# Prompt state of an mLSTM mixer in chunks of two token tiles, and v split in two parts where it is made

## Chip, cores and metric

The kernel runs on one core of one Trainium2 chip as a single launch. The metric is device time in microseconds (us), the median of several executions. TensorE (PE) multiplies matrices, VectorE (DVE), ScalarE (ACT) and GpSimd (POOL) work on elements, and SyncE (SP) issues most DMA transfers; ACT issues some.

## What is computed

Two layers in f32 over 1024 prompt frames and 8 sample streams of 16 frames, with 1024 model features and an inner width of 2048. Layer 0 is a gMLP-style mixer (A), layer 1 an xLSTM mLSTM block (B) of 4 heads of 512. The change is in mixer B, whose core the reference computes chunk by chunk, with a state C (512 x 512 per head) that is carried on:

```python
q, k, v = blockdiag(xc, wq), blockdiag(xc, wk), blockdiag(xm, wv)
...
s = jnp.einsum('bhtd,bhsd->bhts', q, k) * w_intra
num = jnp.einsum('bhts,bhse->bhte', s, v) + w_inter[..., None] * jnp.einsum('bhtd,bhde->bhte', q, C)
den = jnp.sum(s, axis=-1) + w_inter * jnp.einsum('bhtd,bhd->bht', q, n)
h = num / jnp.maximum(jnp.abs(den), jnp.exp(-m_t))[..., None]
...
C_new = decay[..., None, None] * C + jnp.einsum('bhs,bhsd,bhse->bhde', w, k, v)
n_new = decay[..., None] * n + jnp.einsum('bhs,bhsd->bhd', w, k)
```

Then h is layer-normed, gated by silu(z), and projected back with w_out. Outputs are the frames of both batches and the new states (C, n, m, conv) of both. The length of a chunk is free for the result: a longer chunk moves work from "q times C" to "scores times v".

## The kernel before

**Precision.** Most products are made in three matmuls (mm3) from two parts of each operand: `split(hi, lo, x, eng)` casts x to hi on ACT (L89) and subtracts on DVE or, where named, on POOL (L90). A scores block is a plain f32 matmul, which stands as two records in the profile.

**Stages.** 0 to 820 us: mixer A. 852 to 1147: the feature stage, 16 features of 3 steps; a step makes, for 384 tokens, the inner feature (xmp), the convolution and silu (xc), v in token order (`values`, PSUM tile pvv), q and k, and stores v, skip*xc, q and k into DRAM tensors (vb_d, sk_d, q_d, k_d), all issued by ACT. 1147 to 1173: gate section (rA, transposes with ident). 1173 to 1405: the matmuls of z with the first sample streams. 1405 to 1960: the rest of the unit stage.

**Unit stage.** 36 units: 4 heads x (8 prompt tiles of 128 tokens, and one tile with the 128 sample tokens, a "rider" that shares the iteration of a prompt unit). For a prompt tile n of head h an iteration runs, in PE's order: the two halves (a = 0, 1; 258 and 256 columns) of the numerator, scores times v (`va,s`) and, for n > 1, the scaled q times the state (`Ch,q`, `Cl,q`); the state update k times v (`va,k`) in 4 row blocks c and 2 halves; the scores and transposed k of the next tile (`qT,kT`, `ident,kT`); the output projection of the tile two before (`w,o`, whose sum into the residual x is L1380, on DVE); transposes of the normalised output (`ident,hn`). Between them stand the sample streams: for each of 8 samples and 4 heads a state of 512 x 512 comes from DRAM (c), is read by q (`c,qT`), gets a rank-48 update (`sk`, from the DRAM tensor st_d, which `Dec.keys` writes) and goes back. cw holds the gate weights of a tile; it is loaded by partition broadcast (L1037), and `mask` (L1211) is its first reader.

**State.** Tile 0's update waits for tile 1: these two are already one chunk (k0, `parts`, sO, the tile 1 terms of the code). From tile 2 on each tile is a chunk of its own: Cst = Cst * decay + update (L1278 on DVE, 8 times a tile), and `settle` splits Cst into Ch and Cl, a row block at a time, by ACT with DVE or POOL in turn. v is loaded as f32 (vv) and split into va by `prep_v` (ACT, then POOL). `scale_q` (L1252) multiplies q by the carried-state weight.

**Order.** PE executes in the order of the program; the order on the other engines is set by the scheduler. Buffers: 3 va tiles, 2 k2, one sO (in the q2 pool), one Cst, Ch and Cl.

Of the kernel before, what the change touches and what calls it, by code (L numbers as in the profile page):

```python
# [15 lines left out]
P = 128  # L16
# [7 lines left out]
H = 4  # L24
# [46 lines left out]
def trunk_kernel(ctx: ExitStack, tc: tile.TileContext, ins: dict, outs: list):  # L71
# [56 lines left out]
    vb_d = [dram.tile([NT * P, DH], F32, name=f"vb_d{h}") for h in range(H)]  # L128
# [577 lines left out]
    class Feature:  # L706
# [60 lines left out]
        def values(self, b):  # L767
# [8 lines left out]
            st = bw.tile([P, 3, P], F32, name="st", bufs=5)  # L776
            A.copy(out=st, in_=pvv[:, :, :P])
            V.tensor_tensor(out=gtok[:, 3 * b:3 * b + 3], in0=gtok[:, 3 * b:3 * b + 3], in1=pvv[:, :, P:], op=ALU.add)
            A.dma_start(out=vb_d[h].rearrange("(n p) e -> p n e", p=P)[:, 3 * b:3 * b + 3, fs], in_=st)
            sk = bw.tile([P, BT], F32, name="st", bufs=5)  # L780
# [67 lines left out]
    def z_steps():  # L848
        for f in range(NF):
# [3 lines left out]
            for b in range(NB):  # L853
# [3 lines left out]
                st = zs.tile([P, BT], F32, name="st", bufs=5 if zs is bw else 2)  # L857
# [129 lines left out]
    dec8 = const.tile([SB, H], F32, name="dec8")  # L987
    selh = gt.tile([H, H, P], F32, name="selh")
    V.tensor_copy(out=selh, in_=ident[:H, :H].unsqueeze(2).to_broadcast([H, H, P]))
    tpd, tp8 = (ps.tile([P, DH], F32, name="sm") for _ in range(2))  # L990
    for h in range(H):
        T.matmul(tpd[:, 16 * h:16 * h + 16], selh[:, h], de16, start=True, stop=True)
    T.transpose(tp8[:SB, :H], de16[:, 8:16], ident[:H, :H])
    V.tensor_copy(out=decB.rearrange("p h c -> p (h c)"), in_=tpd[:, :16 * H])
    V.tensor_copy(out=dec8, in_=tp8[:SB, :H])

    k0 = const.tile([P, H], F32, name="k0")
    V.tensor_tensor(out=k0, in0=tok[:, 0, 1], in1=decB[:, :, 1], op=ALU.mult)
# [19 lines left out]
    def load_qkv(pool, h, n, want, prev=None, bufs=None):  # L1018
# [10 lines left out]
        if "v" in want:  # L1029
            t = pool.tile([P, DH], F32, name="vv")  # L1030
            l = S.dma_start(out=t, in_=vb_d[h][ts, :])
            if prev is not None:
                after(l, prev)
            got["v"] = t
# [17 lines left out]
    class Dec:  # L1052


        def __init__(self, h, prev):
            self.h = h
            self.g = load_qkv(dw, h, 8, ("qT",), prev, bufs=2)
            self.g.update(load_qkv(dw, h, 8, ("cw",), prev))
            self.ev = []
            kv = self.kv = rawp.tile([P, 2, DH], F32, name="raw")  # L1060
            loads = (S.dma_start(out=kv[:, 0].rearrange("p (c t) -> p c t", c=DC), in_=k_d[h].rearrange("(c p) t -> p c t", p=P)[:, :, 8 * P:]),
                     S.dma_start(out=kv[:, 1], in_=vb_d[h][8 * P:, :]))
            for l in loads:
                if prev is not None:
                    after(l, prev)
            self.nn = dw.tile([SB, DH], F32, name="nn")
            S.dma_start(out=self.nn, in_=ins["state_mlstm_n"][0, :, h])
# [5 lines left out]
        def keys(self):  # L1073
# [6 lines left out]
            kp = k_tokens(self.kv[:, 0].rearrange("p (c t) -> p c t", c=DC), ps, "sm")  # L1080
            kw = self.kw = rawp.tile([P, DH], F32, name="raw")
            A.activation(out=kw, in_=kp, func=AF.Copy, scale=tok[:, 8, 1, h:h + 1])
            kv = wp.tile([P, 4, DH], F32R, name="w")
            split(kv[:, 0], kv[:, 1], kw, G)
            split(kv[:, 2], kv[:, 3], self.kv[:, 1], G)
            for r, (kpart, vpart) in enumerate(((0, 2), (0, 3), (1, 2))):
                for q, part in enumerate((kpart, vpart)):
                    S.dma_start(out=f32(st_d[h])[:, r * SL:(r + 1) * SL, q, :], in_=f32(kv)[:, part])
# [4 lines left out]
        def normaliser(self):  # L1093
            h = self.h
            pn = ps.tile([P, DH], F32, name="sm")
            T.matmul(pn[:SB], blk8, self.kw, start=True, stop=True)
            V.scalar_tensor_tensor(out=self.nn, in0=self.nn, scalar=dec8[:, h:h + 1], in1=pn[:SB], op0=ALU.mult, op1=ALU.add)
            A.dma_start(out=n_s[0, :, h, :], in_=self.nn)
# [60 lines left out]
    vas = [me.tile([P, 2, 2, VA], F32R, name=f"va{j}", bufs=1) for j in range(3)]  # L1159
# [8 lines left out]
    class Unit:  # L1168
        def __init__(self, h, n):
            self.h, self.n, self.smp = h, n, n == 8  # L1170
            self.inter = 1 < n < 8
            self.g = {}
# [12 lines left out]
    def scores_pe(u):  # L1185
# [15 lines left out]
        if u.n == 1:  # L1201
# [4 lines left out]
    def mask(u, step):  # L1206
# [5 lines left out]
        else:  # L1212
            e = A.activation(out=u.dd, in_=u.dd, func=AF.Exp, bias=tok[:, u.n, 0, u.h:u.h + 1])
            if u.n == 2:
                after(e, u.before.sO_split)

    def prep_k(u):
# [3 lines left out]
        col = tok[:, u.n, 1, u.h:u.h + 1] if u.n else k0[:, u.h:u.h + 1]  # L1221
# [3 lines left out]
    def prep_s(u):  # L1225
# [7 lines left out]
        if u.n == 1:  # L1233
# [354 lines left out]
```

## Time and profile before

| | before |
|---|---|
| median of 3 runs, us | 1967.85 (1966.57 to 1975.25) |
| profiled execution, us | 1961.52 |
| its span on the core, us | 1959.8 |
| mean granted TensorE clock, share of full speed | 0.986 |
| PE busy, us of the span | 1900.5 (97%) |
| DVE / ACT / POOL busy, us | 1270.3 / 850.0 / 621.4 |
| DMA | 328.21 MB, mean 167 GB/s |

The profile is one execution, so sums are made against its 1961.52 us. PE busy counts matmul records, which overlap in a pipeline; the distance between the starts of two groups is what a group costs.

### The profile page before, as it was taken

What the parts mean: (1) busy time and instruction counts of PE and PEld (TensorE: products, weight loads), DVE (VectorE), ACT (ScalarE), POOL (GpSimd) and SP (SyncE); (2) the same over time, 40 slices, a digit from 0 to 9 for tenths busy, and PEclk for the clock granted to TensorE, in tenths of its full rate; (3) what the DMA queues carried; (4) which work ended last, traced back from release to release, by engine and by line L of the source; (5) the groups of instructions that cost most, each with busy time, mean ns of one, the idle gap of its engine ahead of it and who ended that gap; (6) DMA issues with size and microseconds to landing.
All of it is one profiled execution on the core that took longest, in us unless ns stands there. A gap on an engine that the chain in (4) does not pass through costs nothing.

```text
span 1959.8 us, 32037 instructions
## 1 busy us (share of the span) xinstructions
PE 1900.5 (97%) x11553; PEld 1681.2 (86%) x11553; DVE 1270.3 (65%) x2522; ACT 850.0 (43%) x1727; POOL 621.4 (32%) x637
## 2 busy tenths in 40 slices
PE   7999999999998999989999989999999999999998
PEld 6888999999998788889999959888987787788887
DVE  5822477777776354477667635222498798898897
ACT  5422444444444243455555635112343344344454
POOL 3000244444441000035444401000145435345466
PEclk9999999999999999999999979999999999999999
DMA  6222333333334654335555554687998897775533
GB/s 213 92 92 77 106 98 103 103 103 99 103 98 163 200 170 142 113 99 154 161 162 156 167 152 143 207 259 235 282 306 264 267 284 243 261 239 177 154 122 129
DMA packets 345690, 328.21 MB, mean 167 GB/s; under 512 B 28164, under 2 KB 276948, under 8 KB 345532
## 3 DMA queue, kind: packets, MB, share of 16 engines
q1 hardware_dynamic: 288812, 261.03, 43.3%
q10 hardware_dynamic: 56720, 65.13, 10.6%
q8 instruction: 91, 1.49, 0.3%
q14 instruction: 67, 0.55, 0.1%
HBM read 203.07 MB, written 123.02 MB: 166 GB/s over the span
## 4 chain that ended last, share of the span: by engine, by line
PE 74%; DVE 13%; DMA 7%; ACT 2%; issue 2%; POOL 1%; SPq 1%; ACTq 0%; POOLq 0%; DVEq 0%
PE sm L58 74%; DVE Cst L1278 2%; DMA cw<-cw_d 2%; DVE c L1129 2%; DVE Cl L90 1%; DVE qT L1252 1%; DMA out<-c 1%; DVE raw L1361 1%; DVE bst L1318 1%; DMA c<-in_state_mlstm_C 1%; DMA vv<-vb_d 1%; DMA r<-in_a_w_in 0%; DVE dn L1324 0%; DVE x L1380 0%; DMA st_d<-w 0%
## 5 line engine op out<-in xcount | busy, mean ns | idle before, releaser
L58 PE MATMUL sm<-xh,w 128*128 128x384 f32 x1536 | 410.9, 341 | 4.3 <-DVE w L90 1.5
L58 PEld LDWEIGHTS sm<-xh,w 128*128 128x128 f32 x1536 | 281.5, 189 | 12.8 <-issue 8.2
L58 PE MATMUL sm<-xl,w 128*128 128x384 f32 x768 | 260.4, 339 | 1.1 <-DVE xl L90 1.1
L58 PE MATMUL sm<-Xh,w 128*128 128x288 f32 x1024 | 216.3, 298 | 4.6 <-ACT c L499 4.6
L58 PE MATMUL sm<-w,o 128*128 128x512 f32 x864 | 209.9, 398 | 2.9 <-ACT o L89 1.2
L58 PE MATMUL sm<-w,os 128*128 128x512 f32 x864 | 200.7, 393 | 6.6 <-ACT os L89 6.6
L58 PEld LDWEIGHTS sm<-w,os 128*128 128x128 f32 x864 | 162.9, 190 | 42.8 <-ACT os L89 9.1
L58 PEld LDWEIGHTS sm<-w,o 128*128 128x128 f32 x864 | 159.8, 188 | 41.1 <-ACT hn L1330 1.7
L58 PE MATMUL sm<-w,Xh 128*128 128x512 f32 x576 | 180.2, 394 | 1.8 <-DVE w L90 1.4
L58 PEld LDWEIGHTS sm<-Xh,w 128*128 128x128 f32 x1024 | 168.2, 189 | 5.2 <-ACT c L499 5.0
L90 DVE TENSOR_TENSOR w<-r,w 128x512 fp32r<-128x512 f32 x176 | 136.1, 779 | 50.3 <-ACT w L89 49.8
L58 PE MATMUL sm<-S,w 128*128 128x288 f32 x1152 | 163.8, 297 | 0.0
L90 DVE TENSOR_TENSOR w<-raw,w 128x1024 fp32r<-128x1024 f32 x44 | 56.4, 1281 | 156.8 <-ACT w L89 156.7
L58 PEld LDWEIGHTS sm<-S,w 128*128 128x128 f32 x1152 | 155.1, 188 | 0.8
L58 PE MATMUL sm<-Xl,w 128*128 128x288 f32 x512 | 151.4, 296 | 0.0
L58 PEld LDWEIGHTS sm<-xl,w 128*128 128x128 f32 x768 | 145.1, 189 | 1.3 <-DVE xl L90 1.3
L89 ACT CAST w<-r 128x512 fp32r<-128x512 f32 x176 | 107.3, 618 | 68.8 <-PE sm L58 29.3
L58 PEld LDWEIGHTS sm<-w,Xh 128*128 128x128 f32 x576 | 108.0, 189 | 25.3 <-DVE w L90 2.6
L58 PE MATMUL sm<-w,Xl 128*128 128x512 f32 x288 | 112.6, 391 | 0.0
L90 DVE TENSOR_TENSOR os<-or,os 128x384 fp32r<-128x384 f32 x96 | 53.0, 556 | 90.1 <-ACT os L89 90.1
L58 PE MATMUL sm<-va,k 128*128 128x258 f32 (+1 forms) x768 | 104.5, 286 | 3.4 <-DVE x L1380 1.7
L89 ACT CAST w<-raw 128x1024 fp32r<-128x1024 f32 (+1 forms) x56 | 55.2, 987 | 116.6 <-DMA raw<-in_b_w_in 91.2
(306 smaller groups left out, 3734.5 us busy)
## 6 DMA issues: line engine op xcount, KB each, us to landing
c<-in_state_mlstm_C SPq DMA_DIRECT2D x64, 512.0 KB
out<-c SPq DMA_DIRECT2D x64, 512.0 KB
r<-in_a_w_in SPq DMA_DIRECT2D x96, 256.0 KB
or<-o_d SPq DMA_DIRECT2D x96, 192.0 KB
raw<-in_b_w_in SPq DMA_DIRECT2D x32, 512.0 KB
qT<-q_d SPq DMA_DIRECT2D x40, 256.0 KB
vh<-v_d SPq DMA_DIRECT2D x48, 192.0 KB
vb_d<-st ACTq DMA_DIRECT2D x48, 192.0 KB
```

Source lines behind the costliest of these rows:

```text
L58: ins = fn(*args, **kw)
L89: first = A.copy(out=hi, in_=src)
L90: (lo_eng or V).tensor_tensor(out=lo, in0=src, in1=f32(hi), op=ALU.subtract)
L1129: V.scalar_tensor_tensor(out=c0[:, cc], in0=c0[:, cc], scalar=decB[:, d.h, 8 + b:9 + b], in1=pc, op0=ALU.mult, op1=ALU.add)
L1252: V.tensor_tensor(out=u.g["qT"], in0=u.g["qT"], in1=u.g["cw"][:, 1:2].to_broadcast([P, DC, P]), op=ALU.mult)
L1278: V.scalar_tensor_tensor(out=Cst[:, c, a, :w], in0=Cst[:, c, a, :w], scalar=decB[:, h, n:n + 1], in1=pc, op0=ALU.mult, op1=ALU.add)
L1318: V.bn_stats(out=bst[:, a], in_=hn[:, a, :256])
L1361: V.scalar_tensor_tensor(out=og[:, c], in0=u.pT[:, c], scalar=colB[:, HNG, 4 * h + c:4 * h + c + 1], in1=g["sk"][:, c], op0=ALU.mult, op1= ...
```

## The change

On odd tiles (n = 1, 3, 5, 7) the unit also computes an off-diagonal score block O, this tile's q with the k of the tile before, and adds O times that tile's v to its numerator. The state is updated, and split into Ch and Cl, on odd tiles alone, from both tiles' k and v. So each chunk has two tiles, as tiles 0 and 1 had. q of an odd tile is scaled by the decay of the tile before as well. v is split into its two parts in the feature stage, right out of PSUM (tile sv), stored as two parts (vb_d gets a leading 2) and loaded by two DMAs straight into va, of which there are four; `prep_v` and the vv tile go. `Dec.keys` copies v's parts into st_d without a split. The sample normaliser is made transposed, in n0T, with one final transpose.

```diff
-    vb_d = [dram.tile([NT * P, DH], F32, name=f"vb_d{h}") for h in range(H)]
+    vb_d = [dram.tile([2, NT * P, DH], F32R, name=f"vb_d{h}") for h in range(H)]
...
-            st = bw.tile([P, 3, P], F32, name="st", bufs=5)
-            A.copy(out=st, in_=pvv[:, :, :P])
+            sv = bw.tile([P, 2, 3, P], F32R, name="sv", bufs=2)
+            split(sv[:, 0], sv[:, 1], pvv[:, :, :P])
...
-            A.dma_start(out=vb_d[h].rearrange("(n p) e -> p n e", p=P)[:, 3 * b:3 * b + 3, fs], in_=st)
-            sk = bw.tile([P, BT], F32, name="st", bufs=5)
+            for q in range(2):
+                A.dma_start(out=f32(vb_d[h])[q].rearrange("(n p) e -> p n e", p=P)[:, 3 * b:3 * b + 3, fs], in_=f32(sv)[:, q])
+            sk = bw.tile([P, BT], F32, name="st", bufs=3)
...
-    dec8 = const.tile([SB, H], F32, name="dec8")
...
-    tpd, tp8 = (ps.tile([P, DH], F32, name="sm") for _ in range(2))
+    tpd = ps.tile([P, DH], F32, name="sm")
...
-    T.transpose(tp8[:SB, :H], de16[:, 8:16], ident[:H, :H])
...
-    V.tensor_copy(out=dec8, in_=tp8[:SB, :H])
-    k0 = const.tile([P, H], F32, name="k0")
-    V.tensor_tensor(out=k0, in0=tok[:, 0, 1], in1=decB[:, :, 1], op=ALU.mult)
+    k0 = const.tile([P, 4, H], F32, name="k0")
+    for j in range(4):
+        V.tensor_tensor(out=k0[:, j], in0=tok[:, 2 * j, 1], in1=decB[:, :, 2 * j + 1], op=ALU.mult)
+    dec2 = const.tile([P, H, 4], F32, name="dec2")
+    d2 = decB[:, :, 0:8].rearrange("p h (j i) -> p h j i", i=2)
+    V.tensor_tensor(out=dec2, in0=d2[:, :, :, 0], in1=d2[:, :, :, 1], op=ALU.mult)
...
-            t = pool.tile([P, DH], F32, name="vv")
-            l = S.dma_start(out=t, in_=vb_d[h][ts, :])
-            if prev is not None:
-                after(l, prev)
-            got["v"] = t
+            va = got["v"] = vas[0]
+            vas.append(vas.pop(0))
+            for q in range(2):
+                S.dma_start(out=f32(va)[:, q, :, :256], in_=f32(vb_d[h])[q, ts, :].rearrange("p (a e) -> p a e", a=2))
...
-            kv = self.kv = rawp.tile([P, 2, DH], F32, name="raw")
-            loads = (S.dma_start(out=kv[:, 0].rearrange("p (c t) -> p c t", c=DC), in_=k_d[h].rearrange("(c p) t -> p c t", p=P)[:, :, 8 * P:]),
-                     S.dma_start(out=kv[:, 1], in_=vb_d[h][8 * P:, :]))
+            self.kT = rawp.tile([P, DC, P], F32, name="raw")
+            self.vv = rawp.tile([P, 2, DH], F32, name="raw")
+            loads = (S.dma_start(out=self.kT, in_=k_d[h].rearrange("(c p) t -> p c t", p=P)[:, :, 8 * P:]),
+                     S.dma_start(out=self.vv, in_=f32(vb_d[h])[:, 8 * P:, :].rearrange("q p e -> p q e")))
...
-            self.nn = dw.tile([SB, DH], F32, name="nn")
-            S.dma_start(out=self.nn, in_=ins["state_mlstm_n"][0, :, h])
...
-            kp = k_tokens(self.kv[:, 0].rearrange("p (c t) -> p c t", c=DC), ps, "sm")
-            kw = self.kw = rawp.tile([P, DH], F32, name="raw")
+            kp = k_tokens(self.kT, ps, "sm")
+            kw = self.kw = self.kT.rearrange("p c t -> p (c t)")
...
-            kv = wp.tile([P, 4, DH], F32R, name="w")
+            kv = wp.tile([P, 2, DH], F32R, name="w")
...
-            split(kv[:, 2], kv[:, 3], self.kv[:, 1], G)
-            for r, (kpart, vpart) in enumerate(((0, 2), (0, 3), (1, 2))):
-                for q, part in enumerate((kpart, vpart)):
-                    S.dma_start(out=f32(st_d[h])[:, r * SL:(r + 1) * SL, q, :], in_=f32(kv)[:, part])
+            for r, (kpart, vpart) in enumerate(((0, 0), (0, 1), (1, 0))):
+                for q, src in enumerate((f32(kv)[:, kpart], self.vv[:, vpart])):
+                    S.dma_start(out=f32(st_d[h])[:, r * SL:(r + 1) * SL, q, :], in_=src)
...
         def normaliser(self):
...
-            pn = ps.tile([P, DH], F32, name="sm")
-            T.matmul(pn[:SB], blk8, self.kw, start=True, stop=True)
-            V.scalar_tensor_tensor(out=self.nn, in0=self.nn, scalar=dec8[:, h:h + 1], in1=pn[:SB], op0=ALU.mult, op1=ALU.add)
-            A.dma_start(out=n_s[0, :, h, :], in_=self.nn)
+            pn = ps.tile([P, DC, SB], F32, name="sm")
+            for c in range(DC):
+                T.matmul(pn[:, c], self.kw[:, c * P:(c + 1) * P], blk8, start=True, stop=True)
+            nv = n0T[:, :, :, h]
+            V.tensor_tensor(out=nv, in0=nv, in1=decB[:, h, 8:16].unsqueeze(1).to_broadcast([P, DC, SB]), op=ALU.mult)
+            V.tensor_tensor(out=nv, in0=nv, in1=pn, op=ALU.add)
+            if h == H - 1:
+                pt = ps.tile([P, P], F32, name="sm")
+                T.transpose(pt, n0T.rearrange("p c b h -> p (c b h)"), ident)
+                no = rawp.tile([P, P], F32, name="raw")
+                V.tensor_copy(out=no, in_=pt)
+                A.dma_start(out=n_s[0].rearrange("b h (c p) -> c (b h) p", p=P), in_=no)
...
-    vas = [me.tile([P, 2, 2, VA], F32R, name=f"va{j}", bufs=1) for j in range(3)]
+    vas = [me.tile([P, 2, 2, VA], F32R, name=f"va{j}", bufs=1) for j in range(4)]
...
-        if u.n == 1:
+        if u.odd:
...
                 T.matmul(u.pO, u.before.g["kT"][:, c], g["qT"][:, c], start=(c == 0), stop=(c == DC - 1))
...
-            if u.n == 2:
+            if u.n in (2, 4, 6):
...
-        col = tok[:, u.n, 1, u.h:u.h + 1] if u.n else k0[:, u.h:u.h + 1]
+        col = tok[:, u.n, 1, u.h:u.h + 1] if u.odd else k0[:, u.n // 2, u.h:u.h + 1]
...
-        if u.n == 1:
+        if u.odd:
...
-            V.scalar_tensor_tensor(out=dO, in0=u.pO, scalar=tok[:, 0, 1, u.h:u.h + 1], in1=u.g["cw"][:, 1], op0=ALU.mult, op1=ALU.mult)
-            u.sO = mw.tile([P, 2, DC, P], F32R, name="q2", bufs=1)[:, :, 0]
+            V.scalar_tensor_tensor(out=dO, in0=u.pO, scalar=tok[:, u.n - 1, 1, u.h:u.h + 1], in1=u.g["cw"][:, 1], op0=ALU.mult, op1=ALU.mult)
+            u.sO = mw.tile([P, 2, P], F32R, name="sO", bufs=1)
...
-    def prep_v(u):
-        if u is None:
-            return
-        va = u.va = vas[0]
-        vas.append(vas.pop(0))
-        vv = u.g["v"].rearrange("p (a e) -> p a e", a=2)
-        split(va[:, 0, :, :256], va[:, 1, :, :256], vv, G)
...
     def scale_q(u):
...
-        V.tensor_tensor(out=u.g["qT"], in0=u.g["qT"], in1=u.g["cw"][:, 1:2].to_broadcast([P, DC, P]), op=ALU.mult)
+        cw = u.g["cw"][:, 1:2].to_broadcast([P, DC, P])
+        if u.odd:
+            V.scalar_tensor_tensor(out=u.g["qT"], in0=u.g["qT"], scalar=decB[:, u.h, u.n - 1:u.n], in1=cw, op0=ALU.mult, op1=ALU.mult)
+        else:
+            V.tensor_tensor(out=u.g["qT"], in0=u.g["qT"], in1=cw, op=ALU.mult)
...
     def update(u, c):
...
-        if u.smp or n == 0:
+        if not u.odd:
...
-            parts = (u.before, u) if n == 1 else (u,)
+            parts = (u.before, u)
...
-                mm3(pc, v.k2[:, 0, cs], v.k2[:, 1, cs], v.va[:, 0, a, :w], v.va[:, 1, a, :w], v is parts[0], v is u)
+                mm3(pc, v.k2[:, 0, cs], v.k2[:, 1, cs], v.g["v"][:, 0, a, :w], v.g["v"][:, 1, a, :w], v is parts[0], v is u)
...
             else:
-                V.scalar_tensor_tensor(out=Cst[:, c, a, :w], in0=Cst[:, c, a, :w], scalar=decB[:, h, n:n + 1],
+                V.scalar_tensor_tensor(out=Cst[:, c, a, :w], in0=Cst[:, c, a, :w], scalar=dec2[:, h, n // 2:n // 2 + 1],
...
     def numerator(u, a):
...
-        va = u.va
+        va = u.g["v"]
...
-        mm3(o, u.s2[:, 0], u.s2[:, 1], va[:, 0, a, :w], va[:, 1, a, :w], True, not u.inter and u.n != 1)
-        if u.n == 1:
-            vb = u.before.va
-            mm3(o, u.sO[:, 0], u.sO[:, 1], vb[:, 0, a, :w], vb[:, 1, a, :w], False, True)
+        mm3(o, u.s2[:, 0], u.s2[:, 1], va[:, 0, a, :w], va[:, 1, a, :w], True, not u.inter and not u.odd)
+        if u.odd:
+            vb = u.before.g["v"]
+            mm3(o, u.sO[:, 0], u.sO[:, 1], vb[:, 0, a, :w], vb[:, 1, a, :w], False, not u.inter)
...
     def settle(u, c):
...
-        if u.smp or n == 0:
+        if not u.odd:
...
-        prep_v(nxt)
...
-            prep_v(rid)
```

Three places of the order of instructions, before and after.

**PE, between two prompt units** (head 0; before: the scores of tile 3 and the start of its numerator; va is v, s the scores, c and sk a sample stream's tiles). Before:

```order
L58 MATMUL sm<-qT,kT 128x128 x4
L58 MATMUL sm<-ident,kT 128x128 x4
L58 MATMUL sm<-w,o_14277 128x512 x24
L58 MATMUL sm<-ident,hn 128x128 x4
L58 MATMUL sm<-c_14303,qT 32x512 x2
L58 MATMUL sm<-c_14305,qT 32x512 x2
L58 MATMUL sm<-sk_14301 128x512 x4
L58 MATMUL sm<-va_12456,s_14432 128x258 x3
L58 MATMUL sm<-Ch,q_14438 128x258
L58 MATMUL sm<-Cl,q_14438 128x258
```

After, at the same place:

```order
L58 MATMUL sm<-qT,kT 128x128 x4
L58 MATMUL sm<-ident,kT 128x128 x4
L58 MATMUL sm<-qT,kT 128x128 x4
L58 MATMUL sm<-w,o_14370 128x512 x24
L58 MATMUL sm<-ident,hn 128x128 x4
L58 MATMUL sm<-c_14396,qT 32x512 x2
L58 MATMUL sm<-c_14398,qT 32x512 x2
L58 MATMUL sm<-sk_14394 128x512 x4
L58 MATMUL sm<-va_12556,s_14480 128x258 x3
L58 MATMUL sm<-va_12555,sO 128x258 x3
L58 MATMUL sm<-Ch,q_14489 128x258
L58 MATMUL sm<-Cl,q_14489 128x258
```

A second qT,kT group, the block O, follows the transposes of k, and the numerator begins with a second group of three on the va of the tile before, from sO.

**ACT, in the feature stage** (head 1; from the cast of v in the last step of one feature into the next step). Before, st is the copy of v out of PSUM that the vb_d store takes:

```order
L777 COPY st<-sm 128x384
L796 COPY qk<-sm 128x384 x2
L779 DMA vb_d_103<-st 128x3x128
L782 DMA sk_d_107<-st 128x384
L798 DMA q_d_95<-qk 64x2x384
L798 DMA k_d_99<-qk 64x2x384
L760 ACTIVATE xc<-xc 128x384
L745 COPY xmp<-sm 128x384
L89 CAST xc_9955<-xc 64x384 x2
L777 COPY st<-sm 128x384
L796 COPY qk<-sm 128x384
```

After, sv is v's high part:

```order
L89 CAST sv<-sm 128x384
L783 DMA sk_d_107<-st 128x384
L797 COPY qk<-sm 128x384 x2
L780 DMA vb_d_103<-sv 128x3x128
L799 DMA q_d_95<-qk 64x2x384
L799 DMA k_d_99<-qk 64x2x384
L780 DMA vb_d_103<-sv 128x3x128
L745 COPY xmp<-sm 128x384
L760 ACTIVATE xc<-xc 128x384
L89 CAST sv<-sm 128x384
```

The copy became a cast into sv, the one vb_d store became two, the second of which stands behind the issues of q and k, and the copy of xmp now stands ahead of the silu (L760).

**SP, at the start of the gate section** (bgc is a small gate bias; c tiles are states of sample streams). Before:

```order
L892 DMA bgc<-in_b_b_gates 4x2x1
L894 DMA m0T<-in_state_mlstm_m 4x8x1
L1025 DMA qT<-q_d_94 128x4x128
L1067 DMA nn<-in_state_mlstm_n 8x512
L1111 DMA c_12628<-in_state_mlstm_C 128x2x512
L1111 DMA c_12630<-in_state_mlstm_C 128x2x512
L1111 DMA c_12716<-in_state_mlstm_C 128x2x512
L1111 DMA c_12718<-in_state_mlstm_C 128x2x512
L144 DMA raw<-in_b_w_in 128x8x128 x2
L1037 DMA cw<-cw_d 128x2x128
```

After:

```order
L893 DMA bgc<-in_b_b_gates 4x2x1
L895 DMA m0T<-in_state_mlstm_m 4x8x1
L1027 DMA qT<-q_d_94 128x4x128
L1118 DMA c_12728<-in_state_mlstm_C 128x2x512
L1118 DMA c_12730<-in_state_mlstm_C 128x2x512
L1118 DMA c_12816<-in_state_mlstm_C 128x2x512
L1118 DMA c_12818<-in_state_mlstm_C 128x2x512
L1027 DMA qT<-q_d_94 128x4x128
L1027 DMA kT<-k_d_98 128x4x128
L1027 DMA qT<-q_d_94 128x4x128
L1027 DMA kT<-k_d_98 128x4x128
L1027 DMA sk<-sk_d_106 128x4x128
```

The load of nn is gone, and five loads of q, k and skip stand ahead of the weights of z that came directly behind the c tiles. In both orders bgc stands ahead of the four c loads.

## Rows read from the trace of the kernel before

**Rows 1.** The page's head: busy time of each engine, DMA packets by size.
```profile
PE 1900.5 (97%) x11553; PEld 1681.2 (86%) x11553; DVE 1270.3 (65%) x2522; ACT 850.0 (43%) x1727; POOL 621.4 (32%) x637
...
DMA packets 345690, 328.21 MB, mean 167 GB/s; under 512 B 28164, under 2 KB 276948, under 8 KB 345532
```

**Rows 2.** Stretches: span, each engine's busy time, granted clock, DMA share, GB/s.
```profile
852.00:1147.00 295.00, 292.30 (x1765) 273.72 (x1764) 202.77 (x450) 175.20 (x388) 127.09 (x182) 1.00 0.56 158
1147.00:1173.00 26.00, 18.45 (x55) 6.18 (x55) 7.90 (x20) 1.98 (x3) 0.00 (x0) 0.54 0.49 154
1405.00:1540.00 135.00, 131.01 (x871) 105.08 (x871) 118.12 (x258) 60.69 (x118) 63.79 (x50) 0.99 0.88 282
1405.00:1960.00 555.00, 532.27 (x3467) 442.26 (x3466) 481.25 (x1050) 248.83 (x486) 275.11 (x220) 0.98 0.71 225
```

**Rows 3.** What PE waited for, 1405 to 1960: us, times, longest.
```profile
PE sm L58 <- DVE x L1380: 8.3, 7, 2.7
```

**Rows 4.** What DVE waited for, 1405 to 1960: us, times, longest.
```profile
DVE dd L1211 <- DMA cw<-cw_d: 20.4, 12, 4.2
DVE x L1380 <- PE sm L58: 18.8, 15, 2.1
```

**Rows 5.** Timeline of DVE and PE at one stall: start, us, [idle before].
```profile
1496.26 0.29 DVE L1211 TENSOR_TENSOR dd<-cw,m_pr 128x128 f32<-128x128 f32 x1 [4.19 <-DMA cw<-cw_d]
...
1497.20 0.74 PE L58 MATMUL sm<-sk 48*128 48x512 f32 x1 [2.68 <-DVE x L1380]
```

**Rows 6.** Timeline of PE in the unit stage: groups of alike records.
```profile
1467.65 0.95 PE L58 MATMUL sm<-n0T,qT 128*128 128x8 f32 x8
1468.46 0.63 PE L58 MATMUL sm<-ident,raw 128*128 128x128 f32 x4
...
1481.61 2.36 PE L58 MATMUL sm<-va,k 128*128 128x258 f32 x18
1483.86 1.16 PE L58 MATMUL sm<-qT,kT 128*128 128x128 f32 x8
1484.86 0.60 PE L58 MATMUL sm<-ident,kT 128*128 128x128 f32 x4
1485.39 1.02 PE L58 MATMUL sm<-raw,blk 128*8 128x512 f32 x2
1486.34 5.85 PE L58 MATMUL sm<-w,o 128*128 128x512 f32 x24
```

**Rows 7.** Groups by line and operation, 1405 to 1960: busy, mean ns, idle before.
```profile
L1278 DVE SCALAR_TENSOR_TENSOR Cst<-Cst,decB,sm 128x258 f32<-128x258 f32 x192 | 82.2, 468 | 2.5 <-PE sm L58 2.5
...
L90 DVE TENSOR_TENSOR Cl<-Cst,Ch 128x514 fp32r<-128x514 f32 x48 | 56.5, 1177 | 0.9 <-ACT Ch L89 0.8
...
L90 POOL TENSOR_TENSOR Cl<-Cst,Ch 128x514 fp32r<-128x514 f32 x48 | 70.5, 1469 | 93.3 <-ACT Ch L89 47.2 <-PE sm L58 35.5 <-DMA sk<-st_d 7.4
L90 POOL TENSOR_TENSOR va<-vv,va 128x512 fp32r<-128x512 f32 x33 | 42.4, 1289 | 18.7 <-ACT va L89 18.5
```

**Rows 8.** Feature stage: a wait of ACT, a group of DVE, ACT's store issues.
```profile
ACT xc L760 <- DVE xc L758: 78.9, 43, 2.7
...
L90 DVE TENSOR_TENSOR xc<-xc,xc 64x384 fp32r<-64x384 f32 x96 | 55.6, 579 | 45.8 <-ACT xc L89 43.9
...
L779 ACTq DMA_DIRECT2D vb_d<-st x48: 371/377/392, 853.3 to 1141.8; - x48
```

**Rows 9.** Timeline of PE, DVE, SP and ACT at the gate section's start.
```profile
1154.57 1.44 PE L58 MATMUL sm<-rA,ident 8*4 8x384 f32 x2 [7.55 <-DVE rA L887]
...
1153.97 1.71 DVE L887 COPY rA<-sm 8x384 f32<-8x384 f32 x3 [11.75 <-DMA c<-in_state_mlstm_C]
...
1147.99 6.17 SPq L1111 DMA_DIRECT2D c<-in_state_mlstm_C  x4
...
1148.45 0.61 ACTq L798 DMA_DIRECT2D k_d<-qk  x1
```

**Rows 10.** Timeline of PE at the first sample stream.
```profile
1240.27 1.23 PE L58 MATMUL sm<-sk 48*128 48x512 f32 x4 [2.43 <-DMA sk<-st_d]
```

More of the change, by code (lines that the diff above doesn't have):

```diff
@@ L856, in z_steps @@
                     last = done[NF + f] = mm3(pm, w[:, 0, k], w[:, 1, k], xh[b][:, k], xl[b][:, k], k == 0, k == KD - 1)
-                st = zs.tile([P, BT], F32, name="st", bufs=5 if zs is bw else 2)
+                st = zs.tile([P, BT], F32, name="st", bufs=3 if zs is bw else 2)
                 A.activation(out=st, in_=pm, func=AF.Silu)
@@ L1171, in __init__ @@
             self.inter = 1 < n < 8
+            self.odd = n % 2 == 1
             self.g = {}
@@ L1446, in first_scores @@
         prep_s(u)
-        prep_v(u)
     plan.setdefault(last - 5, []).append(first_loads)
```

## Prediction

> **What bounds the kernel now.** I read the page's head first: TensorE (PE) is busy for 1900.5 us of a span of 1959.8 [rows 1]. That is an average over stages, so the second view is the table of stretches [rows 2]. The change touches three of them. In the feature stage (852 to 1147 us) PE works 292.30 of 295 us, VectorE (DVE) 202.77, ScalarE (ACT) 175.20. In the gate section (1147 to 1173) PE works at a granted clock of 0.54. In the unit stage (1405 to 1960, nearly all of the 32 prompt units) PE works 532.27 of 555 us and DVE 481.25; GpSimd (POOL) and ACT are half idle. So the unit stage has 22.7 us in which PE does nothing, and everything else there is PE work in program order. A PE matmul that is added costs its full length; work that other engines lose pays only through those 22.7 us.
>
> Third view: what PE waited for in the unit stage [rows 3]. The largest entry is the residual sum (x, L1380) on DVE, 8.3 us in 7 waits. Fourth: what DVE itself waited for [rows 4]: 20.4 us for the transfer cw, which no edit shortens. One stall shows both: DVE stood 4.19 us for cw, and the x behind it held PE for 2.68 us [rows 5].
>
> **Added PE work, the first term.** Tiles 3, 5 and 7 of four heads, 12 units, get an off-diagonal score block of four 128x128 f32 matmuls and six more numerator matmuls. Such a block (8 records in the profile) starts at 1483.86 and the next group at 1484.86: 1.00 us [rows 6]. 12 x 1.00 = 12.0 us. The numerator matmuls have the shape of the update's: 18 of them run from 1481.61 to 1483.86, 0.125 us each [rows 6], and 72 x 0.125 = 9.0 us. The update itself keeps its number of matmuls; they move from even units to the odd unit behind. The sample normaliser's one f32 matmul per head (two records, 0.95 us from 1485.39 to 1486.34) becomes four small ones. The nearest is n0T,qT, 8 records in 0.81 us (1467.65 to 1468.46), so the same four cost 0.8 us, and the difference of four heads with the one final transpose is about -0.5 us [rows 6]. Sum: **+20.5 us of PE**, all in a stage where PE is 96% busy. I take +20; the bounds are 18 (numerators at a tighter pitch) and 22.
>
> **Work taken off the others.** The state's multiply-add (Cst, L1278) runs 192 times at 468 ns; half go, 45 us of DVE. The split halves with it: DVE's Cl 24 x 1.177 = 28 us, POOL's 24 x 1.469 = 35; ACT's casts to Ch halve too. The split of v leaves POOL (33 x 1.289 = 42 us here) and ACT [rows 7]. Twelve more dO multiply-adds with their split cost DVE some 4 us, taking a score row's length. DVE falls from 481 to about 410 us.
>
> What is that worth? At most PE's idle 22.7 us and what the half clock behind the longest stalls costs: the window shows 0.98 [rows 2], 2% of 555 us, about 11 us at the very most. Against taking it all: DVE's largest wait is a transfer and stays; the long stalls hang on DVE's position in a chain (score, mask, split, residual), where an even unit loses about 8 x 0.468 + 2 x 1.177 = 6 us of DVE work but an odd unit, which is not relieved, keeps it. So about half the units are helped. I take half of 22.7, **-11.5 us**, and set what the clock gives back against cw, which stays; bounds -5 (some half of the 8.3 us for x, with nothing else) and -28 (nearly all of the idleness and half of the clock).
>
> **Feature stage.** ACT's copy of v becomes a cast of like length; DVE gains 48 subtractions of 128x384 out of PSUM, nearest row 579 ns [rows 8], 28 us in 295. ACT issues a second store per step, 0.38 us each (48 x 0.377) [rows 8], and it must wait for the subtraction. Neither is on PE's path now: DVE has 92 us of slack, and ACT waited 78.9 us for DVE, 43 times [rows 8], which shows that the two already form a loop just short of PE's pace. The order of ACT shows the copy of xmp now ahead of the silu, which shortens that loop; the second store behind DVE's subtraction lengthens it. I take **+1 us**; bounds 0 and +8 (0.17 us in each of 48 steps).
>
> **Gate section and first sample stream.** PE stands 7.55 us before the gates' transposes at 1154.57, because DVE's rA came at 1153.97 after 11.75 us of idleness [rows 9]. The view names a C transfer; I read it as the last feature stores (ACT issues the last one at 1148.45), whose packets share the engines with the four 512 KB loads of C that SP starts issuing at 1147.99 [rows 9]. In the new order the small bgc load, ahead of these C loads in SP's queue, waits for memory those same stores read, so the C loads come later and do not compete: about -2.5 us (0 to -3.5). The first stream made PE wait 2.43 us for st_d at 1240.27 [rows 10]; its v parts no longer need a cast and a subtraction: about -1 (0 to -4). Together **-3.5 us**.
>
> **Transfers.** v is stored and read in two parts: 256 KB more per unit, 9.4 MB more each way over 36 units. In 1405 to 1540 the DMA engines are 88% busy at 282 GB/s [rows 2]. Eight units bring about 2.1 MB there, 7.4 us at that rate, into 16 us of slack. v's pieces fall from 2 KB (512 numbers of a row) to 1 KB. A load that lands later hits cw and so DVE. I take **+2 us**; bounds 0 and +10.
>
> The Trainium skill (Perfetto Trace Analysis, DMA Optimizations) warns that transfers under 2 KB have a large overhead each. By that rule the transfer term would lie at its upper bound, +10, and the sum at +16. The trace does not bear that out so far: of 345690 packets 276948 are under 2 KB already [rows 1], and the busiest stretch still reaches 282 GB/s.
>
> **The sum.** +20 - 11.5 + 1 - 3.5 + 2 = **+8 us**. On the profiled execution's 1961.52 us that is 1969.5. That execution lies 6.3 us under the median of the runs, 1967.85, so on the median it is **1976 us**, +0.4%.
>
> **Rivals.**
> *(a) PE is the bound throughout and the stalls don't shrink.* The waits hang on cw and on the odd units, whose DVE work is untouched; extra transfers add some. For it: DVE's 20.4 us for cw [rows 4] and PE's 1900.5 us [rows 1]. Against it: seven waits for x stand behind DVE's queue. With -5 for the stalls, +3 for the transfers, +1 for the feature stage and -1 for the gate: 20 - 5 + 3 + 1 - 1 = +18, 1986 us.
> *(b) DVE is the limiter and PE merely looks busy: the other side.* If the stalls give their full -28 and the gate and first stream their full -7.5, then with +20, +1 and 0 for transfers: about -14, 1954 us. It decides if DVE's removed 73 us (45 + 28) stand in front of the x that PE waits for. For it: DVE is at 87% in the stage and PE's largest wait is on it. Against it: in front of the same x DVE stood for PE, 18.8 us in 15 waits [rows 4], so the two alternate and DVE is not the only one that is late.
> The Trainium skill (Perfetto Trace Analysis, Identifying the Most-Contended Engine) says that matmul busy time says little of TensorE's headroom and that the share of weight loading should be read: 442.26 of 555 us here, 80%, less than DVE's 87%. By that rule DVE is the more contended engine and (b) would hold.
> I give it less because the added matmuls have a measured pitch, at which they are issued back to back [rows 6]; there is no room inside those rows.
> *(c) The feature stage becomes bound by the loop of ACT and DVE.* The sv tile has two buffers, and ACT, in order, now stands for a DVE subtraction before its second store; the xmp copy of the next step stands behind it. At 0.3 us a step it costs 48 x 0.3 = +14 in place of +1, the sum +21, 1989 us. For it: ACT's 78.9 us of waits for DVE. Against it: those waits cost PE nothing so far (2.7 us idle in 295).
>
> **Chances.** My forecast 0.50, its own range 1967 to 1983; (a) 0.22; (b) 0.20; (c) 0.08. Half a per cent is 9.8 us, about what a measurement of this kernel can tell from no change (its three runs span 8.7 us). Faster by more (under 1958.0): most of (b), 0.17. Slower by more (over 1977.7): (a), (c) and 0.14 of my own case, which lies close to the border: 0.44. Within: the rest, 0.39. The range leaves out half of (b) below and a part of (a) and (c) above: 1957 to 1988 us.
>
> **What would show it.** PE busy in the unit stage up by about 20 us, with as many matmuls as the sum counts; DVE there near 410 us; PE's idle time there near 12 us. If it stays near 22, (a) holds; near zero with the clock at 1.0, (b). In the feature stage the distance between the first and last step should grow by no more than 1 us; if PE idles there, by waits for ACT's xmp or xc, (c) holds. In the gate section the stall before rA should be about 5 us. My prediction is wrong if new waits for va or kT loads appear in PE's list, because SP's queue holds two va loads behind a PE update, or if the odd unit's longer run of matmuls starves its successor of PSUM.

## Result and the profile after

The change made the kernel slower: 1992.17 us median (1983.79 to 1999.38, 4 runs) against 1968.74 us (4 runs), ratio 1.0115, 95% interval 1.0087 to 1.0143, about 23 us. The forecast was 1976 us with a range to 1988. The profiled execution has a span of 1985.7 us.

The page's head of the changed kernel (busy us, share of the span, instructions; then packets):

```profile
PE 1921.1 (97%) x11745; PEld 1706.4 (86%) x11745; DVE 1208.1 (61%) x2473; ACT 806.1 (41%) x1651; POOL 516.7 (26%) x585
...
DMA packets 379807, 348.10 MB, mean 175 GB/s; under 512 B 29448, under 2 KB 315224, under 8 KB 379648
```

PE is 20.6 us busier than in [rows 1], DVE 62 us less, and 20 MB more are moved. The table of stretches, set to about the same points of the program as [rows 2] (the feature stage begins 5 us later, the unit stage 9: its first `va,s` group starts at 1405.16 us before and at 1414.57 after, so that the last two rows begin 1.4 us earlier in the program):

```profile
857.00:1152.00 295.00, 291.62 (x1739) 270.12 (x1738) 223.17 (x495) 173.67 (x386) 116.69 (x183) 0.99 0.69 187
1157.00:1183.00 26.00, 20.79 (x64) 8.36 (x64) 8.96 (x22) 4.19 (x5) 0.00 (x0) 0.61 0.73 205
1413.00:1549.00 136.00, 131.58 (x898) 109.55 (x897) 92.41 (x224) 48.19 (x95) 39.09 (x36) 0.99 0.92 288
1413.00:1986.00 573.00, 546.77 (x3657) 463.50 (x3655) 400.54 (x945) 208.35 (x415) 187.63 (x173) 0.98 0.75 234
```

The unit stage takes 573 us in the table where it took 555 (571.2 and 554.6 from its first `va,s` group to the end of the span). PE is busy for 14.5 us more, and 26.2 us are without PE work where there were 22.7. DVE lost 80.7 us of work there, and PE's idleness did not shrink. What PE waited for in the unit stage, and what DVE waited for (us, times, longest):

```profile
PE sm L58 <- ACT dd L1221: 6.8, 1, 6.8
PE sm L58 <- DVE x L1383: 5.5, 1, 5.5
PE sm L58 <- ACT o L89: 4.0, 2, 2.8
```

```profile
DVE x L1383 <- PE sm L58: 67.0, 45, 2.4
DVE dd L1219 <- DMA cw<-cw_d: 36.4, 14, 8.9
```

Against [rows 3] the seven short waits for x are gone; two long ones stand in their place. Against [rows 4] DVE now stands for PE in front of x 45 times, for 67.0 us: it is early nearly everywhere. But its wait for cw grew from 20.4 to 36.4 us. The longer of its waits, in the timeline of SP, then DVE and PE (start, us, idle before):

```profile
1619.04 2.03 SPq L1138 DMA_DIRECT2D out<-c  x2
1627.37 0.38 SPq L1118 DMA_DIRECT2D c<-in_state_mlstm_C  x1
1627.84 0.97 SPq L1027 DMA_DIRECT2D kT<-k_d  x2
1628.90 0.46 SPq L1118 DMA_DIRECT2D c<-in_state_mlstm_C  x1
1629.45 1.20 SPq L1035 DMA_DIRECT2D va<-vb_d  x2
1630.70 0.59 SPq L1038 DMA_DIRECT2D cw<-cw_d  x1
```

```profile
1637.30 0.29 DVE L1219 TENSOR_TENSOR dd<-cw,m_pr 128x128 f32<-128x128 f32 x1 [8.94 <-DMA cw<-cw_d]
```

```profile
1638.24 0.79 PE L58 MATMUL sm<-sk 48*128 48x512 f32 x1 [5.48 <-DVE x L1383]
```

SP stands from 1621 to 1627 before a c load, then issues two c halves, two kT and v's two parts, 2 MB, and cw last. cw is read 6.6 us after its issue began, the x behind it on DVE comes late, and PE stops for 5.48 us. It is the chain of [rows 5], with a second kT and v's second part ahead of cw. The 6.8 us wait for dd has cw behind it too (issued at 1780.70, read by DVE at 1788.43).

Part of this is the particular execution of before that was profiled. The same kernel, profiled again (before_again, below), has these for its unit stage: the row of the stretch, PE's largest wait and DVE's wait for cw:

```profile
1409.00:1970.00 561.00, 534.47 (x3465) 443.79 (x3464) 482.09 (x1050) 248.96 (x486) 274.15 (x220) 0.98 0.70 223
```

```profile
PE sm L58 <- DVE x L1380: 9.9, 7, 4.0
DVE dd L1211 <- DMA cw<-cw_d: 25.0, 15, 5.5
```

Held against it, the change's unit stage is 9.6 us longer (561.5 us there), not 16.5, and PE's idleness is the same (26.5 and 26.2 us). What stands against both profiles is that the idleness did not shrink and that DVE's wait for cw grew.

The gate section's stall (PE) is 5.21 us where [rows 9] had 7.55, the first stream's 2.05 where [rows 10] had 2.43. bgc is issued late and the four C loads start behind it:

```profile
1162.33 1.44 PE L58 MATMUL sm<-rA,ident 8*4 8x384 f32 x2 [5.21 <-DVE rA L888]
...
1250.29 1.77 PE L58 MATMUL sm<-sk 48*128 48x512 f32 x4 [2.05 <-DMA sk<-st_d]
```

```profile
1161.67 0.27 SPq L893 DMA_DIRECT2D bgc<-in_b_b_gates  x1
...
1162.87 2.00 SPq L1118 DMA_DIRECT2D c<-in_state_mlstm_C  x4
```

### The profile page after: what moved, and what is told of

The parts are those of the page before. It is cut to its first block, busy times and chain, and to the rows that moved or that the text cites. A ratio compares the mean times of both kernels' runs of the same rounds, so it can differ in the third digit from the quotient of the medians.

```text
span 1985.7 us, 32325 instructions
## 1 busy us (share of the span) xinstructions
PE 1921.1 (97%) x11745; PEld 1706.4 (86%) x11745; DVE 1208.1 (61%) x2473; ACT 806.1 (41%) x1651; POOL 516.7 (26%) x585
## 4 chain that ended last, share of the span: by engine, by line
PE 86%; DMA 6%; DVE 4%; issue 1%; ACT 1%; SPq 1%; POOL 0%; ACTq 0%; POOLq 0%; DVEq 0%
PE sm L58 86%; DMA cw<-cw_d 1%; DMA va<-vb_d 1%; DMA sk<-st_d 1%; DMA raw<-vb_d 0%; DMA out<-c 0%; DMA r<-in_a_w_in 0%; DMA raw<-in_b_w_out 0%; DMA c<-in_state_mlstm_C 0%; DMA x<-in_x_prompt 0%; DMA vh<-v_d 0%; DMA st_d<-w 0%; DVE w L90 0%; DVE xc L758 0%; DMA raw<-in_b_w_in 0%
## 5 line engine op out<-in xcount | busy, mean ns | idle before, releaser
L1136 DVE SCALAR_TENSOR_TENSOR c<-c,decB,sm 128x512 f32<-128x512 f32 x128 | 87.8, 740 | 22.9 <-PE sm L58 21.9
L58 PE MATMUL sm<-va,k 128*128 128x258 f32 (+1 forms) x768 | 97.7, 283 | 0.0
```

Of the source, the lines that this page charges most:

```text
L58: ins = fn(*args, **kw)
L1136: V.scalar_tensor_tensor(out=c0[:, cc], in0=c0[:, cc], scalar=decB[:, d.h, 8 + b:9 + b], in1=pc, op0=ALU.mult, op1=ALU.add)
```

## Experiments

Three theories. W: the loss is PE's added work. B: it is the added bytes of v. Q: it is the order of SP's queue, in which cw stands last. Each kernel was timed beside the kernel before on one chip; one thousandth of the ratio is 2 us. The last three columns are of each kernel's one profiled execution: its time, the length of its unit stage (from the first `va,s` group to the end of the span), and DVE's wait for cw there. The kernel before has 1961.52, 554.6 and 20.4 us. One execution can lie several us from the median, so the ratio decides what a kernel costs, and the last columns say where.

| kernel | median us | ratio to before, 95% interval | profiled us | unit stage us | wait for cw us |
|---|---|---|---|---|---|
| the change | 1992.17 | 1.0115 (1.0087 to 1.0143) | 1987.47 | 571.2 | 36.4 |
| cw_on_act | 1981.82 | 1.0054 (1.0038 to 1.0070) | 1983.66 | 571.5 | 22.3 |
| change_half_load | 1981.27 | 1.0060 (1.0037 to 1.0083) | 1982.50 | 568.3 | 31.9 |
| no_offdiag | 1986.93 | 1.0076 (1.0053 to 1.0099) | 1991.32 | 565.9 | 66.5 |
| chunks_only | 1983.95 | 1.0068 (1.0041 to 1.0096) | 1991.34 | 569.1 | 32.9 |
| chunks_no_offdiag | 1973.64 | 1.0012 (0.9997 to 1.0027) | 1974.80 | 557.2 | 39.1 |
| chunks_cw_on_act | 1972.57 | 1.0009 (0.9992 to 1.0026) | 1972.97 | 554.4 | 19.2 |
| v_split_only | 1987.95 | 1.0094 (1.0071 to 1.0116) | 1987.21 | 567.9 | 42.3 |
| vsplit_one_dma | 1983.19 | 1.0063 (1.0041 to 1.0086) | 1991.23 | 570.4 | 45.4 |
| vsplit_cw_on_act | 1978.81 | 1.0025 (1.0014 to 1.0037) | 1977.92 | 567.5 | 40.6 |
| vsplit_half_load | 1973.46 | 0.9993 (0.9976 to 1.0011) | 1974.00 | 559.2 | 33.9 |
| before_cw_on_act | 1966.24 | 0.9965 (0.9953 to 0.9977) | 1965.59 | 555.5 | 20.1 |
| before_again | 1972.20 | 0.9993 (0.9978 to 1.0009) | 1972.10 | 561.5 | 25.0 |

**cw_on_act.** In `load_qkv`:

```diff
-            l = S.dma_start(out=t, in_=cw_d[h, :, ts].partition_broadcast(P))
+            l = (S if pool is dw else A).dma_start(out=t, in_=cw_d[h, :, ts].partition_broadcast(P))
```

> The changed kernel (1992 us median) with the loads of cw for the prompt and sample tiles issued by ACT, not by SP; the same bytes, the same matmuls. Theory Q (queue): the long stalls of PE in the unit stage (5.5 and 6.8 us) come from cw, which SP issues last behind two c halves, two kT and v's two parts, some 2 MB, after it has stood for a store of c; with cw out of that queue both stalls and the half clock behind them go, 12 to 18 us: 1974 to 1980 us, and DVE's wait for cw falls from 36 us to under 15. Theory B (bytes): the DMA engines are full, so cw is late whoever issues it: 1987 to 1997 us, DVE's wait for cw still above 25 us. Theory W (work): the 24 us are nearly all added PE work, stalls of before and after about equal: 1988 to 1994 us.

It gains 0.6%, some 12 us, by intervals that lie apart; its 1981.82 us is 2 us outside Q's range. DVE's wait for cw falls to 22.3 us, not under 15. PE now waits for other transfers of the same burst:

```profile
PE sm L58 <- DMA kT<-k_d: 5.1, 2, 4.0
PE sm L58 <- DMA c<-in_state_mlstm_C: 4.3, 1, 4.3
```

So half of the loss goes when cw leaves SP's queue. The profile doesn't show the way: its unit stage is as long as the change's (571.5 and 571.2 us), though DVE waits 14 us less for cw. The other half of the loss stays.

**chunks_only and v_split_only**: each half of the change alone (the first with `prep_v`, vv and the f32 vb_d of before; the second with the units' code of before, but va loaded directly).

> The changed kernel with v as before: one f32 copy is stored, loaded as vv and split by ACT and POOL in the unit stage (three va tiles); the two-tile chunks and the transposed normaliser stay. Theory Q: 0.25 MB less stands ahead of cw in a unit and no va load waits in SP's queue for an update, so the stalls shrink in part: 1978 to 1986 us. Theory B: the added 9.4 MB each way are gone, so all DMA stalls return to those of before: 1972 to 1980 us. Theory W: the matmuls are the same, 1988 to 1994 us.

> The kernel before (1968.7 us median) with v split in the feature stage, stored and loaded in two parts, and the normaliser made transposed; the chunks stay as before. Theory W: no added PE work but for the feature stage, ACT and POOL relieved: 1962 to 1970 us. Theory Q: one kT at a time stands ahead of cw, v's second part makes it 0.25 MB later: 1968 to 1976 us. Theory B: as many added bytes as the whole change: 1975 to 1985 us.

Each alone is slower, by 0.7% (in Q's range) and 0.9% (above every range); together 1.15%, less than the sum. The v split adds no matmuls to the units but those of the normaliser and takes work off POOL and ACT, so W cannot explain its 18 us. DVE waited 42.3 us for cw there.

**no_offdiag and chunks_no_offdiag.** O is left out for tiles 3, 5 and 7, in the change and in chunks_only:

```diff
-        if u.odd:
+        if u.n == 1:
             u.pO = ps.tile([P, P], F32, name="sm")
```

(and likewise where dO, sO and their products are made).

> The changed kernel without the off-diagonal block of tiles 3, 5 and 7: its 48 f32 matmuls, 72 numerator matmuls, and the dO products and splits are left out (this part of the scores is missing from the output). Loads, update and splits of the state are those of the change. Theory W: PE loses 20 us of work, all of it on the path: 1970 to 1974 us, stalls as in the change. Theory Q and B: iterations get shorter while the transfers stay, so a part of the 20 us comes back as stalls: 1976 to 1984 us.

> chunks_only (1984 us, v as before) without the off-diagonal block of tiles 3, 5 and 7 (that part of the scores is missing from the output): the matmuls are as many as before, Cst and its splits are halved, the bytes are those of before. If the chunks' cost is PE's added work (Theory W for this part): PE 20 us shorter, and DVE's relief shows: 1962 to 1970 us, under the kernel before (1972). If the chunks cost by their loads (kT in pairs, later, in front of cw): 1976 to 1984 us.

Taking some 19 us of matmuls out again gains 8 us in the change (1986.93 us is above every range; the intervals overlap) and 11 in chunks_only (between the two ranges). A part returns as waits: without O, DVE stands for cw longer, which fits transfers that stay as they are while the iterations get shorter. DVE's wait in no_offdiag, to be held against 36.4 in the change:

```profile
DVE dd L1219 <- DMA cw<-cw_d: 66.5, 20, 8.0
```

And chunks_no_offdiag, with nearly the matmuls of before and 58 us less DVE work (1212.0 us busy), is not faster than before; its unit stage takes 557.2 us, where the two profiles of before have 554.6 and 561.5. So the relief of DVE by itself was worth nothing that shows.

**before_again**, the kernel before unchanged.

> The kernel before once more, unchanged, for its scatter. If the 5 us that the changed kernels lose in mixer A and the 3 us up to the first feature, whose code the change does not touch, belong to the profiled execution of before (1961.5 us, 10 us under the median of its later runs), this profile has the first features at 852 to 857 us and the first gsum at 880 to 886 us; if they belong to the change, at 849.5 and 877.5 us. Ratio 1.000 within 0.002.

The groups of gsum matmuls, of which each feature step has some, in before, before_again and the change (first and last start):

```profile
L58 PE MATMUL sm<-xc,gsum x96: 486/488/490, 877.5 to 1140.7; 128*8 128x384 f32 x96
```

```profile
L58 PE MATMUL sm<-xc,gsum x96: 486/488/490, 877.9 to 1142.0; 128*8 128x384 f32 x96
```

```profile
L58 PE MATMUL sm<-xc,gsum x96: 486/488/490, 886.0 to 1150.9; 128*8 128x384 f32 x96
```

From the first group to the last it is 263.2, 264.1 and 264.9 us. The ratio is 1.000 within 0.002, as expected. The span of before_again is 1970.4 us: the execution on which the prediction was made is 10.6 us short of another of the same kernel. By its first gsum the change had lost 8.5 us, before_again 0.4; the other profiles have it from 880.1 us (vsplit_cw_on_act) to 886.3 (no_offdiag).

The 8.5 us are two things. All profiles have the same 5100 PE records up to the first gsum. The record that starts at 852.0 us before starts at 854.0 in before_again, 855.8 in before_cw_on_act and 857.3 in the change, and from 851.7 to 857.9 in the other changed kernels. So 5.3 of the change's 8.5 us lie ahead of that record, nearly all of them in mixer A, whose code is the same; and two kernels without the change differ by 3.8 us there. By the expectation's reading it would belong to the change, as before_again starts early; before_cw_on_act speaks against that, and it isn't shown. The other 3.3 us lie between that record and the first gsum. There PE waits 1.18 us for the xmp copy where it waited 0.23, in a row of three short stops, and behind them the change's clock is at the lower of its two levels, 1.2 GHz (two `xh,w` matmuls take 0.84 us in place of 0.51) until about 878. The wait in question, before and after:

```profile
863.98 0.24 PE L58 MATMUL sm<-ident,cst 24*128 24x24 f32 x1 [0.23 <-ACT xmp L745]
```

```profile
870.10 0.24 PE L58 MATMUL sm<-ident,cst 24*128 24x24 f32 x1 [1.18 <-ACT xmp L745]
```

The stretch, before, in before_again and after:

```profile
850.00:900.00 50.00, 47.47 (x291) 44.49 (x290) 36.31 (x78) 31.25 (x69) 23.11 (x34) 1.00 0.48 136
```

```profile
850.00:900.00 50.00, 48.94 (x301) 45.93 (x300) 36.23 (x76) 30.86 (x69) 23.33 (x35) 1.00 0.47 136
```

```profile
850.00:900.00 50.00, 46.62 (x272) 43.49 (x271) 37.80 (x84) 27.45 (x60) 21.67 (x34) 0.93 0.47 133
```

The clock of this stretch is 0.93 or 0.97 in all ten other kernels that have a part of the change, and 1.00 in the three profiles without. From the record at 852.0 to the last gsum the stage takes 287.9 to 288.9 us in those three, 293.6 in the change and 291.5 to 296.0 in the others.

**before_cw_on_act, vsplit_cw_on_act, chunks_cw_on_act**: the edit of cw_on_act in the kernel before and in each half.

> The kernel before with the loads of cw issued by ACT. Theory Q: the queue in front of cw costs before too (DVE waits 20.4 us for cw): 1962 to 1968 us, DVE's wait under 10 us. Theory B: bytes decide, no difference: 1969 to 1973 us.

> v_split_only (1988 us) with the loads of cw issued by ACT. Theory Q: its 16 us come through cw (DVE waited 42 us for it): 1970 to 1976 us. Theory B: the second part's bytes slow every transfer, c and sk too: 1982 to 1988 us.

> chunks_only with the loads of cw issued by ACT. If what remains of the chunks' cost is PE's work, the gain is that which the kernel before had from the same edit, 6 us: 1975 to 1980 us, 8 to 14 us over before_cw_on_act (1966). If the chunks' cost is cw standing behind pairs of kT: 1966 to 1972 us.

All gain, by intervals that lie apart: 7 us before (in Q's range), 14 us with the v split (between the two ranges), 12 us with the chunks (half a us above the range for cw). A shorter wait of DVE is seen only in the last. It is 20.1 us in before_cw_on_act, where the two profiles of before have 20.4 and 25.0 and under 10 was expected; and 40.6 us in vsplit_cw_on_act, where v_split_only has 42.3, with a unit stage that is as long (567.5 and 567.9). With cw in ACT's queue SP no longer stands for cw's buffer either (before, 15.9 us in 13 waits for `scale_q` alone), and these runs don't tell the two apart. In chunks_cw_on_act the relief that the prediction counted on is there to see, in PE's waits and in the row of the unit stage:

```profile
PE sm L58 <- DVE n0T L1100: 1.8, 1, 1.8
PE sm L58 <- DVE x L1393: 1.7, 1, 1.7
PE sm L58 <- ACT o L89: 1.2, 1, 1.2
```

```profile
1414.00:1971.00 557.00, 543.43 (x3663) 459.54 (x3661) 424.72 (x945) 225.51 (x450) 237.76 (x208) 1.00 0.72 225
```

With all the chunks' matmuls the stage takes 557 us where [rows 2] have 555 and before_again 561, PE idles 13.6 us in place of 22.7 and 26.5, and the granted clock reads 1.00 in place of 0.98. DVE's wait for cw is 19.2 us, 32.9 in chunks_only. This kernel is as fast as the one before; against before_cw_on_act, which has the same order of cw, the chunks cost some 9 us (by ratios taken on two chips). The fastest of all is before_cw_on_act, 0.35% under the kernel before.

**vsplit_half_load, change_half_load**: v's second part is not loaded and is zero (its share is missing from the output).

```diff
-            for q in range(2):
+            for q in range(1):
                 S.dma_start(out=f32(va)[:, q, :, :256], in_=f32(vb_d[h])[q, ts, :].rearrange("p (a e) -> p a e", a=2))
```

> v_split_only with the load of v's second part left out in the unit stage (that part is zero, so the output lacks its share); both parts are still made and stored. Bytes and SP issues of loads return to those of before, the va loads still wait in SP's queue for matmuls that read their buffer. Theory B: 1972 to 1977 us. Theory Q by the wait of the va load, not by its bytes: 1982 to 1988 us. If the loss is in the feature stage's stores: above 1984 us, with the unit stage as in before.

> The changed kernel with the load of v's second part left out in the unit stage (that part is zero, its share is missing from the output). If the second part's load costs here what it cost alone (v_split_only against vsplit_half_load, 15 us): 1976 to 1980 us. If PE's added work leaves the transfers more time, so that the costs do not add (chunks_only 12 and v_split_only 16 make 28, the change has 21): 1982 to 1986 us, as chunks_only.

Alone, the second load carries the whole cost of the v split: 1.0094 falls to 0.9993, 20 us for 36 loads of 256 KB, as B forecast; the unit stage falls from 567.9 to 559.2 us. The second store and the 48 subtractions in the feature stage show no cost in the time, though the stage is some 3 us longer than before (292.0 us from the record at 852.0). In the change the load carries about 11 of 23 us (1.0115 to 1.0060, by the intervals 4 to 18), between the two ranges.

**vsplit_one_dma**: the two parts side by side in vb_d, one DMA of 512 KB for both.

```diff
-    vb_d = [dram.tile([2, NT * P, DH], F32R, name=f"vb_d{h}") for h in range(H)]
+    vb_d = [dram.tile([NT * P, 2, DH], F32R, name=f"vb_d{h}") for h in range(H)]
...
+            S.dma_start(out=f32(va).rearrange("p q a e -> p (q a) e")[:, :, :256], in_=f32(vb_d[h])[ts].rearrange("p q (a e) -> p (q a) e", a=2))
```

> v_split_only (1988 us) with v's two parts side by side in a row of vb_d, so that one DMA of 512 KB loads both: the same bytes, and the same 1 KB pieces on the side of the va tile, half as many issues in SP's queue. If the bytes cost: 1984 to 1991 us. If SP's second issue (0.6 us, in front of cw) costs: 1974 to 1980 us.

1.0063 against 1.0094, with intervals that overlap, 1 us under the range for the bytes: a third of the cost may be SP's second issue; the larger part stays with the bytes and their 1 KB pieces.

## Why the prediction was wrong

**PE's added work (+20).** Right on PE itself. The counts held: 96 records of qT,kT and 72 numerator matmuls more. Added up from start to start without the waits, they take 9.5 and 9.3 us in the change's trace, 12.0 and 9.0 in the sum; the normaliser saved 0.1 us, 0.5 in the sum. PE's busy time in the unit stage rose by less, 14.5 us, as other groups got shorter (`va,k` by 3.4 us, `ev,selm` by 3.0). What didn't hold is that such a matmul costs the kernel its full length: leaving out O gained 8 us in the change and 11 in chunks_only.

**The relief of the others (-11.5): the first step that failed.** DVE fell to 400.54 us, below the 410 forecast, and the short waits for x vanished. The step set the clock's gain "against cw, which stays". cw did not stay: 20.4 us of waits (25.0 in before_again) became 36.4, PE's idleness was 26.2 us where it had been 22.7 (26.5) instead of 11, and the relief was lost in it. The term was also too large: PE's last group of the kernel before starts at 1947.62 us and takes 4.81, so 7.4 of the 22.7 us lie behind the last matmul, where no relief reaches. That the relief existed is shown by chunks_cw_on_act (13.6 us of idleness, clock 1.00), where PE's added work cost some 9 us in place of 19. That cw's place is what took it in the change too is argued from its longest waits: in cw_on_act the profile's unit stage did not get shorter.

**Transfers (+2): the second step that failed.** I set 7.4 us of bytes against 16 us of idle DMA time in the busiest stretch, an average. In the stalls shown above it is the burst behind a freed buffer that counts: SP issues it all at once, and what it issues last comes late. The second load cost about 11 us in the change and 20 us alone (half_load), at and outside the upper bound of 10. The Trainium skill's rule on small transfers (Perfetto Trace Analysis, DMA Optimizations) had put the term at that bound, +10, nearer; but vsplit_one_dma keeps the 1 KB pieces on the va side, so no run here tells the size of the pieces from the bytes.

**Feature stage (+1).** Too small, inside its bounds. From the first gsum to the last it grew by 0.8 to 1.7 us, as forecast. From the record at 852.0 on it grew by 4.9 us (5.7 against before_again), most of it in the stretch at the lower clock ahead of the first gsum. That stretch begins with a longer wait for ACT's xmp, the sign that was named for rival (c); but (c)'s loss in each of the 48 steps did not come.

**Gate section (-2.5) and first stream (-1).** The gate's stall fell by 2.3 us to the 5 us forecast, and by the mechanism that was forecast: bgc is issued at 1161.67 us, the C loads behind it at 1162.87, and DVE's rA comes at 1161.73. The stall is 5.2 us in every kernel with the v split and 7.6 to 9.2 in those without. The first stream gained 0.4.

**The rivals.** (a), 1986 us, came nearest in its mechanism: the stalls did not shrink, and the waits hung on cw; that the odd units went unrelieved is not what the runs point to, and its +3 for transfers was too small. (c)'s 1989 us lies nearer by luck, with a loss in the feature stage that was not there at its size. (b) fell: 80.7 us less DVE work gave no time, and without the added matmuls (chunks_no_offdiag) still none. The Trainium skill's rule (Perfetto Trace Analysis, Identifying the Most-Contended Engine) by which DVE, at 87% against PE's 80% of weight loading, was the one to relieve, did not hold here.

Of its own signs of being wrong, no wait for va or kT loads stands in PE's list for the change; one for kT came in cw_on_act.

Still open: how far the gain of moving cw comes from cw's own place, how far from what stood behind it; what the half of the loss that stays in cw_on_act is made of; and why mixer A takes up to 6 us more in one profile than in another.

## What to carry to other kernels

When work is taken off an engine that waits for transfers, look first at what stands last in the issuing queue's burst and who reads it first; here the relief of the chunks showed only once that transfer had another queue. A share of busy DMA time over a stretch did not price another load; its delay of whatever is issued behind it, from the longest wait of that kind, is a first thing to look at, though no run here tests it as a price. A small transfer that stands last in a long queue is worth a try in another one: that one line gained in all four kernels here, where the change lost. And a sum made against one profiled execution inherits its luck: two executions of the same kernel differed by 10.6 us, more than the effect that was forecast.

## What was unexpected of the hardware

DVE's subtraction to Cl became faster without being touched: 1177 ns in [rows 7], 730 ns in the change, whose POOL works 187.63 us in the unit stage in place of 275.11.

```profile
L90 DVE TENSOR_TENSOR Cl<-Cst,Ch 128x514 fp32r<-128x514 f32 x24 | 17.5, 730 | 0.9 <-ACT Ch L89 0.9
```

Before, single ones ran between 0.68 and 1.79 us. The trace tells them apart by what POOL does when they start. The seven that start while no POOL instruction runs take 0.68 us each; the 41 that start while one runs take 1.26 us in the mean. In the change 15 of the 24 start without one, at 0.68 us. Two of before, the first behind the start of a POOL instruction and the second ahead of it:

```profile
1433.85 1.31 POOL L90 TENSOR_TENSOR Cl<-Cst,Ch 128x514 fp32r<-128x514 f32 x1 [0.90 <-ACT Ch L89]
1433.93 1.77 DVE L90 TENSOR_TENSOR Cl<-Cst,Ch 128x514 fp32r<-128x514 f32 x1
...
1489.48 0.68 DVE L90 TENSOR_TENSOR Cl<-Cst,Ch 128x514 fp32r<-128x514 f32 x1
1489.63 1.69 POOL L90 TENSOR_TENSOR q<-qT,q 128x512 fp32r<-128x512 f32 x1 [1.28 <-ACT q L89]
```

So part of DVE's 80.7 us is not work that was taken away but work that ran faster because POOL had less.
